# Attention steps woven between dense matmuls in a hybrid convolution and attention block on eight cores

## The chip, the cores and the metric

The kernel runs on all 8 cores of one Trainium2 chip, two dies of four cores. Each core computes one of the 8 sequences of the batch by itself; nothing is exchanged between cores. The metric is the device time of the slowest core in microseconds (us). Most executions agree within 0.3%, but this program also has a slower state, in which the cores of one die, or of both, show a lower granted TensorE clock.

Engines are called by their names, and in the profile by short ones: PE is TensorE's matmuls, PEld its weight loads, DVE is VectorE, ACT is ScalarE, POOL is GpSimd.

## The reference

```python
# x: (8, 4096, 1024) float32, one layer
h = rmsnorm(x) * g_mix
b, c, v, q, k, va, gc, ga = split(h @ w_in)          # 512 x 3, 512 x 3, 1024 x 2 columns
y_c = (b * causal_dwconv3(c * v)) @ w_conv_out
# differential attention: 4 heads, each two maps of 64-wide q/k and one 128-wide v
q, k = rope(rmsnorm(q)), rope(rmsnorm(k))
p0, p1 = softmax(mask(q0 k0' / 8)), softmax(mask(q1 k1' / 8))   # causal by chunks of 64
o = rmsnorm((p0 - lam * p1) @ va) * (1 - lam_init)
y_a = o @ w_attn_out
x = x + (sigmoid(gc) * y_c + sigmoid(ga) * y_a) @ w_o
x = x + swiglu(rmsnorm(x) * g_ffn)                   # 1024 -> 2816 -> 1024
```

## The kernel before

Rows go in eight tiles of 512. A tile runs stage by stage: norm, the input projection with the chains that normalise and rotate Q and K, attention, the output projection, feed-forward. Weights are cast from float32 in tile 0, written to device memory in bfloat16, and read from there in tiles 1 to 7. A small scheduler puts a semaphore wait wherever an instruction needs another engine's result; the order on each engine is the order in which the program emits.

Attention stands in one block per tile. For each of 4 heads and each 128-row key tile it issues two score matmuls of 64 rows, two Exps, two PV matmuls (the exponentials times V) with 512 query columns, a matmul with ones for one softmax sum, and a VectorE addition for the other:

```python
for n in range(2):
    S_.op("act", lambda n=n, pi=pi: nc.scalar.activation(
        out=Pb[:, pi, 0:N], in_=banks[sb0 + n][:, 0:N], func=AF.Exp, scale=0.125), ...)
# ... (the next scores but one are issued here)
for n in range(2):
    S_.op("pe", lambda n=n, pi=pi: nc.tensor.matmul(
        banks[n][:, qlo:T], lhsT=Vs[:, kt, h * 128:(h + 1) * 128], rhs=Pb[:, pi, 0:N], ...))
S_.op("pe", lambda p1=p1: nc.tensor.matmul(
    banks[B_L1][:, qlo:T], lhsT=ones[:], rhs=Pb[:, p1, 0:N], start=first, stop=last), ...)
# ... (Lacc[:, 0] += Pb[:, p0] on VectorE)
```

Eight PSUM banks serve everything in turn. The reciprocal square roots of the norms are Ln and Exp on ScalarE, silu and sigmoid are ScalarE functions too, so that activation tables are loaded 33 times.

## Time and profile before

| | before |
|---|---|
| time, median of 3 fast runs | 2957.18 us |
| TensorE busy, of a span of 2953.3 us | 2532.3 us (86%) |
| VectorE, ScalarE, GpSimd busy | 1304.6, 1212.2, 333.9 us |
| mean granted clock, both dies | 0.94 |
| activation table loads in all | 33 |

TensorE is the bound and has 421 us of holes. The prediction below shows them by stretch. The view of TensorE's waits names them (line waited with, what it waited for: us in all, times, longest):

```profile
PE bank L623 <- ACT Pb L637: 63.5, 48, 16.9
PE bank L371 <- DVE xn L361: 52.9, 28, 5.0
PE bank L728 <- DVE mixT L717: 46.2, 8, 6.8
```

These are scores waiting for Exp, transposes waiting for a normalised row, and the attention branch's mix at a stage border. No single one is large; all arise where one stage hands over to the next.

### The profile page before, as it was taken

What the parts mean: (1) busy time and instruction counts of PE and PEld (TensorE: products, weight loads), DVE (VectorE), ACT (ScalarE), POOL (GpSimd) and SP (SyncE); (2) the same over time, 40 slices, a digit from 0 to 9 for tenths busy, and PEclk for the clock granted to TensorE, in tenths of its full rate; (3) what the DMA queues carried; (4) which work ended last, traced back from release to release, by engine and by line L of the source; (5) the groups of instructions that cost most, each with busy time, mean ns of one, the idle gap of its engine ahead of it and who ended that gap; (6) DMA issues with size and microseconds to landing.
All of it is one profiled execution on the core that took longest, in us unless ns stands there. A gap on an engine that the chain in (4) does not pass through costs nothing.

```text
span 2953.3 us, 39312 instructions; the slowest of 8 cores (2940.4 to 2953.3 us)
## 1 busy us (share of the span) xinstructions
PE 2532.3 (86%) x11552; PEld 1036.5 (35%) x11552; DVE 1304.6 (44%) x2186; ACT 1212.2 (41%) x2355; POOL 333.9 (11%) x550
## 2 busy tenths in 40 slices
PE   3758778789887988889898898988989979899888
PEld 1323233244323433234332443223432234332244
DVE  4444234622555144731646225572164641446621
ACT  2453224521382216611385213872138921269620
POOL 1300013000400030000400004000040000400000
PEclk9878889999998999989999999999999989999999
DMA  6757974035312443025310353102531024430033
GB/s 203 253 174 242 327 271 153 33 114 193 123 71 72 170 172 115 27 102 187 140 73 30 116 208 123 53 30 104 187 138 72 1 80 169 165 115 1 29 114 143
DMA packets 58238, 376.06 MB, mean 127 GB/s; under 512 B 6448, under 2 KB 6576, under 8 KB 18352
## 3 DMA queue, kind: packets, MB, share of 16 engines
q1 hardware_dynamic: 44352, 307.49, 30.2%
q10 hardware_dynamic: 9216, 33.56, 3.3%
q0 software_dynamic: 4464, 32.51, 2.6%
q8 instruction: 100, 1.64, 0.2%
q14 instruction: 106, 0.87, 0.1%
HBM read 324.25 MB, written 49.28 MB: 126 GB/s over the span
## 4 chain that ended last, share of the span: by engine, by line
PE 56%; DVE 11%; issue 10%; ACT 8%; DMA 7%; POOL 7%; ACTq 0%; DVEq 0%; POOLq 0%; SPq 0%
PE bank L746 9%; PE bank L751 9%; PE bank L771 9%; PE bank L391 8%; PE bank L651 7%; DMA Vs<-wblk 6%; PE bank L623 5%; ACT Pb L637 5%; POOL scr L465 3%; PE bank L656 3%; PE bank L728 2%; DVE hT L373 2%; POOL scr L461 2%; PE bank L545 2%; DVE scr L714 1%
## 5 line engine op out<-in xcount | busy, mean ns | idle before, releaser
L637 ACT ACTIVATE Pb<-bank 128x512 bf16<-128x512 f32 (+3 forms) x1152 | 565.0, 564 | 49.7 <-PE bank L623 40.1
L663 DVE TENSOR_TENSOR Lacc<-Lacc,Pb 128x512 f32<-128x512 f32 (+3 forms) x544 | 350.8, 645 | 180.0 <-ACT Pb L637 127.0
L391 PE MATMUL bank<-hT,wring 128*128 128x512 bf16 x1792 | 398.8, 384 | 6.3 <-DVE scr L405 3.8
L746 PE MATMUL bank<-hT,wring 128*128 128x512 bf16 x1408 | 348.7, 392 | 22.4 <-DVE hT L373 12.8
L651 PE MATMUL bank<-Pb,Vs 128*128 128x512 bf16 (+3 forms) x1152 | 337.5, 376 | 11.3 <-POOL Pb L641 9.0
L751 PE MATMUL bank<-hT,wring 128*128 128x512 bf16 x1408 | 339.7, 385 | 0.0
L771 PE MATMUL bank<-wring,big 128*128 128x512 bf16 x1408 | 309.5, 381 | 17.1 <-ACT scr L755 7.9
L757 DVE TENSOR_TENSOR big<-bank,scr 128x512 bf16<-128x512 f32 x176 | 120.7, 691 | 453.5 <-PE bank L751 453.5
L623 PE MATMUL bank<-qT,kT 64*128 64x512 bf16 (+3 forms) x1152 | 248.6, 375 | 72.4 <-ACT Pb L637 63.5
L435 PE MATMUL bank<-wring,hT 128*128 128x512 bf16 x768 | 212.2, 433 | 83.1 <-DVE hT L373 23.5
L755 ACT ACTIVATE scr<-bank 128x512 f32<-128x512 f32 x176 | 104.1, 597 | 419.0 <-PE bank L746 418.9
L391 PEld LDWEIGHTS bank<-hT,wring 128*128 128x128 bf16 x1792 | 176.3, 99 | 220.4 <-issue 17.9
L656 PE MATMUL bank<-Pb,ones 128*128 128x512 bf16 (+1 forms) x576 | 212.7, 370 | 0.0
L746 PEld LDWEIGHTS bank<-hT,wring 128*128 128x128 bf16 x1408 | 140.0, 100 | 198.2 <-issue 41.6
L771 PEld LDWEIGHTS bank<-wring,big 128*128 128x128 bf16 x1408 | 137.7, 98 | 187.8 <-issue 25.4
L751 PEld LDWEIGHTS bank<-hT,wring 128*128 128x128 bf16 x1408 | 140.2, 100 | 174.5 <-issue 14.7
L623 PEld LDWEIGHTS bank<-qT,kT 64*128 64x128 bf16 x1152 | 66.2, 93 | 338.6 <-issue 334.1
L457 POOL TENSOR_TENSOR scr<-scr,tabs 128x256 f32<-128x256 f32 x64 | 46.5, 727 | 1151.5 <-DVE ss L452 1151.4
L728 PE MATMUL bank<-wring,mixT 128*128 128x512 bf16 x512 | 131.6, 419 | 46.2 <-DVE mixT L717 46.2
L435 PEld LDWEIGHTS bank<-wring,hT 128*128 128x128 bf16 x768 | 80.2, 109 | 188.5 <-issue 128.7
L641 POOL MEMSET Pb<- 64x64 bf16 x256 | 38.1, 151 | 943.4 <-ACT Pb L637 938.9
L351 ACT ACTIVATE xn<-xt 128x1024 bf16<-128x1024 f32 x36 | 38.0, 1056 | 241.8 <-DVE small L350 241.8
(110 smaller groups left out, 2237.5 us busy)
## 6 DMA issues: line engine op xcount, KB each, us to landing
wring<-wsc SPq DMA_DIRECT2D x217, 1024.0 KB, 5.4
Vs<-wblk SPq DMA_DIRECT2D x62, 1024.0 KB, 12.4
wsc<-wring POOLq DMA_DIRECT2D x31, 1024.0 KB, 12.0
out<-xt ACTq DMA_DIRECT2D x32, 512.0 KB, 7.4
Lacc<-x ACTq DMA_DIRECT2D x28, 512.0 KB, 4.3
xt<-x SPq DMA_DIRECT2D x28, 512.0 KB, 8.5
xt<-x ACTq DMA_DIRECT2D x4, 512.0 KB, 13.6
cst_sb<-cst SPq DMA_DIRECT2D x1, 232.0 KB, 5.6
```

The lines of the kernel that those rows point to most:

```text
L391: S_.op("pe", lambda kc=kc: nc.tensor.matmul(banks[bk][:], lhsT=wv[:, kc, c4 * 128:(c4 + 1) * 128], rhs=hT[:, kc, :], start=(kc == 0), sto ...
L435: S_.op("pe", lambda kc=kc: nc.tensor.matmul(banks[bk][:], lhsT=hT[:, kc, t * 128:(t + 1) * 128], rhs=wv[:, kc, :], start=(kc == 0), stop= ...
L623: S_.op("pe", lambda n=n: nc.tensor.matmul(banks[sb0 + n][:, 0:N], lhsT=kT[n * 64:(n + 1) * 64, h, kt * 128:(kt + 1) * 128], rhs=qT[n * 64 ...
L637: S_.op("act", lambda n=n, pi=pi: nc.scalar.activation(out=Pb[:, pi, 0:N], in_=banks[sb0 + n][:, 0:N], func=AF.Exp, scale=0.125), [("ps", ...
L651: S_.op("pe", lambda n=n, pi=pi: nc.tensor.matmul(banks[n][:, qlo:T], lhsT=Vs[:, kt, h * 128:(h + 1) * 128], rhs=Pb[:, pi, 0:N], start=fir ...
L656: S_.op("pe", lambda p1=p1: nc.tensor.matmul(banks[B_L1][:, qlo:T], lhsT=ones[:], rhs=Pb[:, p1, 0:N], start=first, stop=last), ["ones"] + ...
L663: S_.op("dve", lambda p0=p0: nc.vector.tensor_tensor(out=Lacc[:, 0, qlo:T], in0=Lacc[:, 0, qlo:T], in1=Pb[:, p0, 0:N], op=ALU.add), [("P", ...
L728: S_.op("pe", lambda kc=kc, t=t, bk=bk, wv=wv: nc.tensor.matmul(banks[bk][:], lhsT=mixT[:, kc, t * 128:(t + 1) * 128], rhs=wv[:, kc, :], s ...
L746: S_.op("pe", lambda kc=kc, c2=c2, bg=bg, wv=wv: nc.tensor.matmul(banks[bg][:], lhsT=wv[:, kc, c2 * 128:(c2 + 1) * 128], rhs=hT[:, kc, :], ...
L751: S_.op("pe", lambda kc=kc, c2=c2, bu=bu, wv=wv: nc.tensor.matmul(banks[bu][:], lhsT=wv[:, kc, 256 + c2 * 128:256 + (c2 + 1) * 128], rhs=h ...
L757: S_.op("dve", lambda bu=bu, sg=sg, fi=fi: nc.vector.tensor_tensor(out=big[:, fi, :], in0=banks[bu][:], in1=scr[:, sg, 0:T], op=ALU.mult), ...
L771: S_.op("pe", lambda kc=kc, kl=kl, t=t, c=c, bk=bk, wv=wv: nc.tensor.matmul(banks[bk][:], lhsT=big[:, kc, t * 128:(t + 1) * 128], rhs=wv[: ...
```

## The change

Its intent is to have no attention stage at all. The attention of tile j+1 is cut into steps of one key tile, and a step is put between the dense matmuls of the end of tile j and the start of tile j+1, whenever a credit that grows with every dense matmul reaches one. For that, Q, K and V of tile j+2 are computed in tile j. Chains of other engines (multiply, transpose) are not emitted at once but deferred by so many dense units, a unit being 4 to 8 dense matmuls into one bank.

```diff
+            def mm(fn, reads, writes):
+                S_.op("pe", fn, reads, writes)
+                if st["att"]:
+                    st["credit"] += st["rate"]
+                    while st["credit"] >= 1.0 and st["att"]:
+                        st["credit"] -= 1.0
+                        att_step()
...
+            def unit_end():
+                for e in later:
+                    e[0] -= 1
+                due = [e for e in later if e[0] <= 0]
...                                     # one Exp for both maps; one pair of score banks
-                                out=Pb[:, pi, 0:N], in_=banks[sb0 + n][:, 0:N], func=AF.Exp, scale=0.125),
+                    act(lambda: A.activation(out=Pb[:, pi, :, 0:N], in_=psS[:, :, 0:N], func=AF.Exp, scale=0.125),
...                                     # PV with the queries as rows and a 129th column of ones
-                                banks[n][:, qlo:T], lhsT=Vs[:, kt, h * 128:(h + 1) * 128], rhs=Pb[:, pi, 0:N],
+                                psO[:, b, s * VW:(s + 1) * VW], lhsT=Pb[:, pi, n, (q - r) * 128:(q - r + 1) * 128],
+                                rhs=Vs[:, kt, h * VW:(h + 1) * VW], start=(kt == 0 and s == 0), stop=(kt == 4 * j + q),
...                                     # norms: a power on GpSimd instead of Ln and Exp
+                pool(lambda: G.tensor_tensor(out=rs8, in0=ss8, in1=mhalf[:], op=ALU.pow), [("ss8", pb), "mhalf"], [("rs8", pb)])
...                                     # sigmoid and silu by tanh: one activation table set
-                            out=big[:, gi, :], in_=banks[bk][:], func=AF.Sigmoid,
+                act(lambda: A.activation(out=scr[:, th, 0:T], in_=psD[bk][:], func=AF.Tanh, bias=bgh[:, gi:gi + 1], scale=0.5),
...                                     # the head's epilogue (before fin: reciprocals, the two maps
...                                     # combined on VectorE into wv)
+                    for q in range(4):
+                        act(lambda q=q: A.activation(out=yq[:, yi, q * 128:(q + 1) * 128], in_=wv[:, q, :], func=AF.Square,
+                                                     accum_out=ss[:, q:q + 1]), [("scr", w)], [("yq", yi), ("ess", e)])
...
+                    defer(1, fin)
+                    defer(3, tr)
```

PSUM is divided: one pair of banks for scores, three banks for PV, three for all dense units and transposes. Weights come in half-blocks of 256 columns in place of whole blocks; 6 slots hold them in bfloat16, and 4 staging buffers hold the float32 loads of tile 0 until they are cast.

## The prediction

> **What bounds the kernel now.** I read the table of stretches first, one stretch per 512-row tile; the tile borders are where the chain of waits shows the first normalised rows of a tile being written.
>
> ```profile
> core 4: us, PE busy (x) PEld busy (x) DVE busy (x) ACT busy (x) POOL busy (x), PEclk, DMA share, GB/s
> 0.00:426.00 426.00, 276.43 (x1196) 118.83 (x1196) 167.77 (x276) 151.59 (x230) 57.59 (x102) 0.86 0.74 250
> 426.00:735.00 309.00, 270.19 (x1244) 116.45 (x1244) 129.11 (x226) 101.79 (x210) 39.50 (x64) 0.94 0.35 121
> 2538.00:2953.00 415.00, 372.25 (x1692) 144.24 (x1692) 192.68 (x314) 196.35 (x385) 39.24 (x64) 0.96 0.24 88
> ```
>
> Columns after the length: busy us and count of TensorE matmuls, weight loads, VectorE, ScalarE, GpSimd; granted clock; DMA share and rate. Tile 0 is another regime (DMA 0.74, clock 0.86). Tiles 1 to 7 grow from 309 to 415 us with attention. TensorE is the bound, idle for 2953.3 - 2532.3 = 421 us. The last tile by stage shows where:
>
> ```profile
> 2538.00:2590.00 52.00, 41.12 (x188) 18.20 (x188) 29.59 (x61) 16.73 (x43) 34.53 (x32) 0.91 0.35 130
> 2627.00:2778.00 151.00, 143.63 (x650) 42.88 (x651) 97.05 (x148) 141.52 (x280) 4.70 (x32) 0.99 0.02 7
> 2792.00:2829.00 37.00, 23.51 (x116) 10.51 (x115) 21.61 (x34) 6.22 (x16) 0.00 (x0) 0.84 0.26 96
> 2829.00:2906.00 77.00, 77.00 (x345) 34.39 (x346) 14.53 (x21) 13.82 (x22) 0.00 (x0) 0.97 0.39 137
> ```
>
> Q/K/V (52 us) and output projection (37) have holes and a low clock; attention (151) is ScalarE's, busy 141.5; gate/up (77) is solid, 352 matmuls at 216 ns. Cut into 10 us pieces, the clock is 1.00 except just behind a hole:
>
> ```profile
> 2826.00:2836.00 10.00, 8.04 (x29) 3.51 (x30) 3.05 (x4) 1.88 (x2) 0.00 (x0) 0.59 0.01 2
> 2836.00:2846.00 10.00, 10.00 (x48) 4.51 (x46) 1.72 (x4) 1.79 (x3) 0.00 (x0) 1.00 0.27 105
> ```
>
> Tile 0's late stretch is a chain of weight loads (start, us, what), at a saturated DMA of 330 GB/s (last line, from the table of stretches):
>
> ```profile
> 334.14 13.96 DMA Vs<-wblk
> 348.24 1.91 ACT wring L329
> 350.21 12.46 DMA Vs<-wblk
> ...
> 340.00:380.00 40.00, 26.46 (x110) 10.98 (x109) 8.50 (x10) 10.58 (x11) 2.13 (x4) 0.83 0.99 330
> ```
>
> For the cost of small matmuls and of Exp I read the timeline and the groups by shape:
>
> ```profile
> 1060.30 0.61 PE L371 MATMUL bank<-ident,xn 128*128 128x128 bf16 x8 [0.19 <-DVE xt L779]
> 2700.68 0.65 PE L623 MATMUL bank<-qT,kT 64*128 64x512 bf16 x4
> L637 ACT ACTIVATE Pb<-bank 128x512 bf16<-128x512 f32 x960 | 504.5, 600 | 38.1 <-PE bank L623 35.5 <-DVE Lacc L663 1.3 <-ACT Pb L637 0.8
> L637 ACT ACTIVATE Pb<-bank 128x128 bf16<-128x128 f32 x64 | 14.6, 277 | 9.5 <-PE bank L623 4.6 <-POOL Pb L641 4.1
> L426 ACT ACT_TABLE_LOAD x8 | 10.3, 1283 | 56.3 <-PE bank L391 56.3
> ```
>
> Eight transposes, each with its own weight load, take 0.61 us; less one latency of 219 ns that is 391/7 = 56 ns apiece. Four 64-row QK matmuls take 0.65 us, less 387 ns latency: the fourth starts 0.26 us after the first, so a pair overlaps.
>
> **What the Trainium skill says.**
> - "TensorE: Matmul & The Clock Gate", Back-to-back issue gap: about 81 ns per matmul of 128 columns in a stream with weight loads, 56 ns isolated. The trace has 56 with loads; I use 56.
> - The same page, What's actually happening and Seeing it yourself: the clock halves after about 3.4 us idle, and with three dense cores on a die it falls to 13/16. The trace agrees with the first (0.59 behind a hole) and not the second (1.00 on eight cores).
> - "ScalarE: Activation LUTs", What ACT_TABLE_LOAD costs and Table sets: 186 ns + 0.833 ns per element, 1283 ns per load, exp and tanh in one set. The trace: (600 - 277)/384 = 0.84 ns, 1283 ns. No run yet shows the shared set.
> - "HBM Reference", Specifications: about 358 GB/s per core; the trace tops out near 330.
>
> **The change part by part.**
>
> *TensorE work at full clock.* Dense matmuls stay 976 x 8 = 7808, at 215.7 ns: 1684 us. Removed: the ones matmul of each key tile (480 of 512 columns, 32 each of 384, 256, 128: about 114 us), the fp32 row sum (32 x 0.9 = 29) and the ones matmul of the norm (7), 150 in all. PV turns from 1152 wide matmuls (960 x 0.216 + 64 x (0.162 + 0.109 + 0.056) = 228) into 3584 + 640 = 4224 of 129 columns, at 56 ns 237. QK pairs are now always issued together: 480 x 0.26 (216 ns, and part of the 63 ns by which the second of a pair starts late) + 32 x 0.46 (the three diagonal shapes) = 140. Transposes: 512 + 256 + 128 new ones = 896 x 0.056 = 50. Sum 1684 + 140 + 237 + 50 = 2111 us.
>
> *ScalarE.* One Exp covers both maps: 171 + 0.84 x 1024 = 1.03 us against 2 x 0.6, and 552 us in all (480 x 1.03, 32 x 1.8 for the three diagonal shapes). With the rest (tanh 192, norms and squares 177, copies 115, casts 59) some 1095 us; 32 table loads (41 us) go. No longer a bound, because the Exp is spread over the dense matmuls: in the worst tile, 131 steps over 736 matmuls, one every 5.6. A step plus its dense share is 0.73 + 1.21 = 1.94 us of TensorE, while the single score pair comes free after 0.28 + 0.24 + 1.10 = 1.62 us. Only a tanh in between breaks that: about 15 us in all.
>
> *VectorE.* The row-sum adds (351 us) go; the silu gets a second pass (176 x 0.75 = 132), down is evicted in 192 pieces instead of 64 (+96), the epilogue about 110. I get about 1190 us, 53%: not a bound on average, but in bursts.
>
> *Tile 0 and its prefetch.* 62 half-blocks of 1 MB plus 0.5 MB written back: 1.57/0.328 = 4.8 us each against 3.45 us of matmuls. Setup until the sine tables have gone through DRAM: 42 us. Q/K/V of tiles 0 and 1, paced by VectorE: 2 x 30. Then 52 half-blocks x 4.8 = 249, x tiles 13, bf16 reloads 10, and 10 lost while tile 2's Q/K/V holds the four staging buffers. Together 384, say 385 us. In it TensorE does 1168 dense matmuls (252), attention 0 and most of 1 (24), transposes (13): 289 us.
>
> *The other seven tiles.* 2111 - 289 = 1822 us. At a clock of 0.975 (holes are smaller than now, when tiles show 0.94 to 0.96) 1869 us.
>
> *Stalls that remain.* Three dense banks instead of eight, and VectorE in program order. Per tile with a look-ahead: four normalised transposes ahead of the output projection, evicted at 1.2 us each, 2.5 us; residual and norm, then eight Q/K units of 3.1 us VectorE each (plus 4.9 for the FFN norm) against 2.5 us of TensorE, 10 us; conv taps (3.7 us each) and four norms ahead of the first gated unit, 5.5 us. That is 18, five times outside tile 0: 90. The last two tiles have no Q/K/V to hide the FFN norm: 13 each, 26. With the score pair's 15: 131 us.
>
> *Tail*, last evictions and store: 9, as now. Sum: 385 + 1869 + 131 + 9 = 2394 us, or 0.81 of before.
>
> **The rivals.**
> - *Small PV matmuls cost more than 56 ns* (the skill's 81, or waits on P). For: P is fresh, and weight load and matmul are the same length. Against: the transposes. It adds 4224 x 25 ns = 106 us: 2500.
> - *VectorE becomes the bound*: its bursts and the tiny GpSimd powers, unmeasured, hold the banks. At 2 us a power in norm chains, about 80 more: 2475.
> - *The clock falls* because TensorE is never quiet. Against: 77 us solid at 1.00. At 13/16 the seven tiles would take 1822/0.8125 = 2243: 2770.
> - *Bursts are absorbed* by banks and woven attention, and tile 0 runs nearer its bytes (110 MB at 328 GB/s, 335 us): 345 + 1840 + 60 + 9 = 2254.
> - *Tile 0 is hidden anyway*: then only the weaving counts, and the gain is within these numbers.
>
> **Range and chances.** The fast corner is 2254; stalls of 220 and a clock of 0.95 give about 2540. I take 2270 to 2520. Even the throttled case is 6% faster than 2957, so faster is nearly certain, short of a wait I have missed on the single score pair.
>
> **What would show it right or wrong.** Ones matmuls and row-sum adds gone; PV at about 56 ns start to start; Exp near 1.03 us on 576 instructions; table loads down to a handful; TensorE busy above 93% behind tile 0 with a clock near 0.975; tile 0 ending near 385 us with DMA at 0.9 or more; holes of 10 us in Q/K/V and of 5 at the conv-to-gate border. It is wrong if the clock sits near 0.81, if PV runs at 80 ns, if tile 0 takes over 430 us, or if the waits on VectorE exceed 200 us.

## The result, and the profile after

The changed kernel takes 2863.55 us by the median of four executions. One of these was slow (3089.83); the fast ones are 2845.6, 2860.79 and 2866.3. Ratios here are the mean time of one kernel's fast runs over that of the other's of the same rounds, so not quite the ratio of the medians: 0.966, with a 95% interval of 0.962 to 0.970. It is faster, by 3.4% instead of the predicted 19%; 2394 us and the range up to 2520 were far off.

The page's line of busy times, changed kernel:

```profile
PE 2393.0 (84%) x14080; PEld 1110.5 (39%) x14080; DVE 1159.1 (41%) x2138; ACT 1058.7 (37%) x1556; POOL 243.5 (9%) x239
```

TensorE's work fell by 139 us, and its share fell too: the holes grew from 421 to 451 us. The groups by shape show that the instructions are what they were taken for (count, busy us, mean ns):

```profile
L606 ACT ACTIVATE Pb<-psS 128x1024 bf16<-128x1024 f32 x480 | 490.8, 1023 | 649.0 <-PE psS L600 640.2 <-DVE xt L803 3.0 <-DVE big L829 1.8
...
L411 ACT ACT_TABLE_LOAD x1 | 1.3, 1283 | 7.6 <-DMA xt<-x 7.6
L470 ACT ACT_TABLE_LOAD x1 | 1.3, 1283 | 0.5 <-ACT big L456 0.5
```

One Exp over both maps takes 1.023 us, and two table loads are left. The table of stretches, by tile (length, busy us of TensorE, its weight loads, VectorE, ScalarE, GpSimd, clock, DMA share, GB/s):

```profile
0.00:548.00 548.00, 359.74 (x1757) 159.38 (x1758) 262.26 (x482) 191.05 (x281) 82.22 (x81) 0.86 0.63 204
548.00:868.00 320.00, 275.88 (x1495) 124.83 (x1493) 138.66 (x260) 97.94 (x164) 30.33 (x29) 0.92 0.38 128
...
1910.00:2270.00 360.00, 318.27 (x2112) 151.68 (x2110) 138.64 (x260) 159.72 (x225) 30.33 (x29) 0.97 0.32 106
```

Tile 0 takes 548 us where 385 had been predicted, and its DMA share is 0.63 where 0.9 or more had been. The later tiles have holes and, with them, a clock of 0.92 to 0.97. The waits of TensorE:

```profile
PE psD L666 <- DVE yq L657: 76.0, 19, 5.6
PE psS L600 <- ACT Pb L606: 58.9, 25, 7.6
PE psD L555 <- DVE scr L538: 54.2, 29, 3.4
PE psD L515 <- DVE scr L538: 46.2, 16, 5.1
```

L666 are the transposes that end a head's attention epilogue (its softmax sums divided out, the two maps combined, the row normalised and transposed), L600 the scores, L555 and L515 the transposes and the projection in the Q/K/V stages. All waits for VectorE together are 373 us by this view, against 248 before.

To put these in relation I added up the gaps from one matmul's start to the next on the slowest core: content at full clock (215.8 ns for 512 columns, 56 for 128 and so on), the part of the rest that a lowered clock explains, and waits. Content is 2089 us, clock loss 143, waits 596. The prediction had 2111 of content and 283 for all else; 2089 counts a pair of scores as one matmul, 2111 had 0.26 us for it, which is about the difference. Of the two runs in the last columns the next section tells.

| clock loss and waits, us | predicted | changed kernel | epilogue spread | best |
|---|---|---|---|---|
| tile 0 (with the first Q/K/V stages) | 96 | 249 | 224 | 171 |
| Q/K/V, borders, output projection, tiles 1 to 7 | 116 | 310 | 283 | 174 |
| feed-forward and convolution stages, tiles 1 to 7 | 15 | 180 | 107 | 109 |
| clock, not divided by place | 47 | (above) | (above) | (above) |
| sum | 274 | 739 | 614 | 454 |

The predicted 96 is 385 less 289 of content, 116 is 90 for the look-ahead tiles and 26 for the last two; the tail's 9 is left out of the column.

**Two chains read from the timeline.** The first is the end of a head in tile 2's down projection (start us, us, engine, line):

```profile
1187.26 0.39 PE L600 MATMUL psS<-qT,kT 64*128 64x512 bf16 x2
...
1192.75 0.58 PE L666 MATMUL psD<-ident,yq 128*128 128x128 bf16 x4 [3.92 <-DVE yq L657]
...
1188.43 0.31 ACT L650 ACTIVATE yq<-scr 128x128 bf16<-128x128 f32 x1 [2.74 <-DVE scr L645]
...
1190.22 1.00 ACT L606 ACTIVATE Pb<-psS 128x1024 bf16<-128x1024 f32 x1
...
1190.80 1.01 POOL L654 TENSOR_TENSOR ep<-ep,mhalf 128x4 f32<-128x4 f32 x1 [61.74 <-DVE ep L652]
...
1191.91 0.69 DVE L657 TENSOR_TENSOR yq<-scr,ep 128x512 bf16<-128x512 f32 x1 [0.33 <-POOL ep L654]
```

ScalarE stands 2.74 us in front of the first square (L650), because VectorE is still combining the two maps. The Exp of the scores of 1187.26 is behind the four squares in program order and starts at 1190.22. GpSimd's power ends at 1191.81, VectorE's multiply starts 0.1 us later, and TensorE, which met the transposes (L666) three units after the epilogue, has stood still for 3.92 us. The clock is then reduced: 0.67 in the 4 us that follow, in the table of stretches. The head shown is typical: in the view of ScalarE's waits it stands before the first square at 31 of the 32 heads.

```profile
ACT yq L650 <- DVE scr L645: 104.8, 31, 6.3
```

The second is a Q/K unit of tile 1 on VectorE:

```profile
139.15 0.68 DVE L529 TENSOR_TENSOR scr<-psD,tabs 128x512 f32<-128x512 f32 x1
...
140.61 0.68 DVE L538 TENSOR_TENSOR scr<-psD,tabs 128x512 f32<-128x512 f32 x1
143.70 0.69 DVE L546 TENSOR_TENSOR yq<-scr,st 128x512 bf16<-128x512 f32 x1 [2.41 <-POOL scr L542]
144.31 0.68 DVE L529 TENSOR_TENSOR scr<-psD,tabs 128x512 f32<-128x512 f32 x1
```

The unit's pitch is 144.31 - 139.15 = 5.16 us, of which VectorE stands 2.41 in front of L546, waiting for GpSimd's power (1.64 us) and addition (1.09). The reason is a count: the chain says "after one unit", but it is registered before its own unit ends, so that the multiply is emitted at the end of the same unit.

### The profile page after: what moved, and what is told of

It reads as the page before. It is cut to its first block, busy times and chain, and to the rows that moved or that the text cites. A ratio compares the mean times of both kernels' runs of the same rounds, so it can differ in the third digit from the quotient of the medians.

```text
span 2843.8 us, 41548 instructions; the slowest of 8 cores (2839.7 to 2843.8 us)
## 1 busy us (share of the span) xinstructions
PE 2393.0 (84%) x14080; PEld 1110.5 (39%) x14080; DVE 1159.1 (41%) x2138; ACT 1058.7 (37%) x1556; POOL 243.5 (9%) x239
## 4 chain that ended last, share of the span: by engine, by line
PE 67%; DVE 13%; issue 8%; ACT 4%; POOL 4%; DMA 3%; DVEq 1%; ACTq 0%; POOLq 0%; SPq 0%
PE psD L817 20%; PE psD L698 12%; PE psO L617 10%; PE psD L844 9%; PE psS L600 6%; PE psD L515 4%; PE psD L764 4%; PE psD L791 3%; DMA kT<-wblk 2%; ACT yq L650 2%; POOL scr L542 2%; DVE scr L645 2%; DVE scr L529 2%; DVE st L532 1%; POOL small L415 1%
## 5 line engine op out<-in xcount | busy, mean ns | idle before, releaser
L606 ACT ACTIVATE Pb<-psS 128x1024 bf16<-128x1024 f32 (+1 forms) x576 | 548.1, 952 | 795.5 <-PE psS L600 774.8
L817 PE MATMUL psD<-hF,wring 128*128 128x512 bf16 x2816 | 666.3, 385 | 10.5 <-DVE hF L426 5.0
L698 PE MATMUL psD<-hT,wring 128*128 128x512 bf16 x1792 | 448.0, 395 | 15.9 <-DVE Pb L609 6.9
L817 PEld LDWEIGHTS psD<-hF,wring 128*128 128x128 bf16 x2816 | 267.0, 99 | 294.0 <-issue 30.1
L617 PE MATMUL psO<-Vs,Pb 128*128 128x129 bf16 x4224 | 351.7, 229 | 3.1 <-DVE Pb L609 3.1
L844 PE MATMUL psD<-wring,big 128*128 128x512 bf16 x1408 | 333.3, 383 | 8.3 <-DVE wring L356 7.7
L515 PE MATMUL psD<-wring,hT 128*128 128x512 bf16 x768 | 245.5, 468 | 76.2 <-DVE scr L538 46.2
L617 PEld LDWEIGHTS psO<-Vs,Pb 128*128 128x128 bf16 x4224 | 256.1, 101 | 123.6 <-issue 114.7
L803 DVE SCALAR_TENSOR_TENSOR xt<-psD,xt 128x512 f32<-128x512 f32 x256 | 176.2, 691 | 272.3 <-PE psD L844 214.7
L600 PE MATMUL psS<-qT,kT 64*128 64x512 bf16 (+3 forms) x1152 | 222.1, 382 | 59.0 <-ACT Pb L606 58.9
L600 PEld LDWEIGHTS psS<-qT,kT 64*128 64x128 bf16 x1152 | 56.3, 93 | 315.5 <-issue 315.5
L515 PEld LDWEIGHTS psD<-wring,hT 128*128 128x128 bf16 x768 | 81.4, 114 | 175.1 <-issue 135.2
L791 PE MATMUL psD<-wring,big 128*128 128x512 bf16 x512 | 124.7, 392 | 7.5 <-DVE wring L356 3.6
## 6 DMA issues: line engine op xcount, KB each, us to landing
xt<-x ACTq DMA_DIRECT2D x4, 512.0 KB, 13.6
```

Of the source, the lines that this page charges most:

```text
L515: mm(lambda kc=kc, k4=k4, wv=wv: nc.tensor.matmul(psD[bk][:], lhsT=hT[:, jb, kc, t * 128:(t + 1) * 128], rhs=wv[:, k4, :], start=(kc == 0) ...
L600: S_.op("pe", lambda n=n: nc.tensor.matmul(psS[:, n, 0:N], lhsT=kT[n * 64:(n + 1) * 64, h, kt * 128:(kt + 1) * 128], rhs=qT[n * 64:(n + 1) ...
L606: act(lambda: A.activation(out=Pb[:, pi, :, 0:N], in_=psS[:, :, 0:N], func=AF.Exp, scale=0.125), [("ps", "S")], [("P", pi)])
L617: S_.op("pe", lambda q=q, n=n, b=b, s=s: nc.tensor.matmul(psO[:, b, s * VW:(s + 1) * VW], lhsT=Pb[:, pi, n, (q - r) * 128:(q - r + 1) * 12 ...
L698: mm(lambda kc=kc: nc.tensor.matmul(psD[bk][:], lhsT=wv[:, kc, col * 128:(col + 1) * 128], rhs=hT[:, jb, kc, :], start=(kc == 0), stop=(kc ...
L791: mm(lambda kc=kc, k4=k4, wv=wv, t=t, bk=bk: nc.tensor.matmul(psD[bk][:], lhsT=mixT[:, kc, t * 128:(t + 1) * 128], rhs=wv[:, k4, :], start ...
```

## The experiments

All give correct results but the one that is wrong. "Changed kernel" stands for its fast runs, 2846 to 2866 us, mean 2858.

**The Q/K chain's multiply one unit later.**

```diff
-                defer(1, fin)
-                defer(3, tr)
+                defer(2, fin)
+                defer(4, tr)
```

> Only the Q/K finishing multiply (and its transposes) are put one unit later. In the changed kernel a Q/K unit takes 5.2 us: VectorE runs four operations (0.69+0.68+0.17+0.69), then stands 2.4 us at the finishing multiply until GpSimd has done the power (1.64) and the add (1.1), then 0.69. Theory A (this chain in VectorE's program order is what the Q/K/V stage costs): the pitch falls to about 3.2 us, each of the eight Q/K/V stages of some 62 us to about 42, the first two included, so 2845 becomes 2690 +- 30. Theory B (the three dense banks, which the transposes share, bound the stage anyway): the pitch stays over 4.5 us and the time over 2800. Theory C (tile 0's time is its weight loads, hidden anyway): tiles 1 to 7 gain but tile 0 stays at 548.

Measured: 2766.57 and 2774.24 us (a third run, slow, 2906.32), ratio to before 0.936. VectorE's multiply now follows without a gap:

```profile
138.27 0.68 DVE L538 TENSOR_TENSOR scr<-psD,tabs 128x512 f32<-128x512 f32 x1
138.87 0.68 DVE L546 TENSOR_TENSOR yq<-scr,st 128x512 bf16<-128x512 f32 x1
```

By the places of the matmuls in the traces, the Q/K/V stages of the later tiles went from between 62 and 66 us to between 47 and 51, and the first two together from 129 to 108. So the cause is real, worth 87 us, and about half as large as expected: in these stages TensorE then waited for banks whose evictions stood behind other work of VectorE.

**The norms of the tile after next spread over the gate units.**

```diff
-                        norm_pre(t)
-                for t in range(4):
-                    x_load(j, t)
+                        defer(2 + 3 * t, lambda t=t: (norm_pre(t), x_load(j, t)))
```

> Only the four look-ahead norms, which stand together behind the conv, are spread over the first gated stage, one every three units. In the changed kernel that stage takes 38 us for 23 us of matmuls in tiles 1 to 5. Theory A (VectorE waits in program order for ScalarE's squares and GpSimd's powers, and the gated units' banks wait behind it): the stage falls to about 30 us, 6 x 8 = 50 us in all, so about 2795. Theory B (the stage's holes come from the last head's transposes and the conv taps): under 15 us gain.

Measured: 2850.66 us (and 2900.19, 1.7% above it). A miss: no gain, although the border between convolution and gate had 14 us of waits and clock loss a tile. In its place the trace showed the last head's transposes at that border, 5.5 to 6.1 us, and the convolution taps.

**The weaving undone, all else kept.** After each start of an attention its steps are run one behind the other.

```diff
+                while st["att"]:
+                    att_step()
+                    unit_end()
```

> The weaving undone: all attention steps of a tile one after the other at the same place of the program, everything else as in the changed kernel. A step then costs the loop of the single score pair, about 0.28 + 0.24 + 1.1 = 1.65 us against 0.93 us of TensorE now. Theory (weaving is what carries the gain): 448 full steps x 0.75 us and 128 short ones x 0.4 more, so about 2845 + 390 = 3235, slower than the kernel before. Rival (ScalarE's Exp total is what counts, woven or not, so the stage is as in the kernel before at 1.05 us a step): about 2900.

Measured: 3417.55 us, one run, far slower than the kernel before and 180 us more than the theory expected. The first line of the waits says why:

```profile
PE psS L600 <- ACT Pb L606: 460.5, 509, 6.3
```

With one pair of score banks each step waits for the Exp of the step ahead. So the change's cheaper attention (query-major PV, one Exp) loses without the weaving, and the weaving is worth some 560 us in this kernel with its single pair. Part of that may be order: the edit counts each step as a unit, so that the deferred chains come due among the steps.

**Scores over the full 128 rows, wrong** (both maps' products are added; the result is off by 0.34 relative). It tests whether the step of 0.89 us, predicted as 0.73, comes from the change between 64-row and 128-row matmuls. In the changed kernel a step looks like this:

```profile
1163.88 2.97 PE L844 MATMUL psD<-wring,big 128*128 128x512 bf16 x13
1166.78 0.39 PE L600 MATMUL psS<-qT,kT 64*128 64x512 bf16 x2
1167.10 0.63 PE L617 MATMUL psO<-Vs,Pb 128*128 128x129 bf16 x8
1167.56 2.75 PE L844 MATMUL psD<-wring,big 128*128 128x512 bf16 x12
```

Thirteen dense matmuls at 0.216 us would be through at 1166.69; the scores start 0.1 us later, and PV 0.32 us behind them instead of 0.22.

```diff
-                            psS[:, n, 0:N], lhsT=kT[n * 64:(n + 1) * 64, h, kt * 128:(kt + 1) * 128],
-                            rhs=qT[n * 64:(n + 1) * 64, jb, h, qlo:T], start=True, stop=True),
+                            psS[:, n, 0:N], lhsT=kT[:, h, kt * 128:(kt + 1) * 128],
+                            rhs=qT[:, jb, h, qlo:T], start=True, stop=True),
```

> Wrong results on purpose: the two score matmuls of a step use all 128 rows instead of 64 each (so both maps get the sum of both scores), which takes the pair's overlap away (2 x 216 ns) but also the change between 64-row and 128-row matmuls. Theory A (that change costs about 0.1 us into and 0.1 us out of every pair, as the gaps before the first score matmul and after the second suggest): the two cancel, a step keeps its 0.9 us, total within 30 us of 2845. Theory B (the gaps are waits for the Exp): a step grows by about 0.15 us, 448 steps, total about 2910.

Measured: 2865.17 us, one run, within the stated 30 us: theory A. In its trace the second score matmul starts 216 ns after the first, where it was 3 ns, so the overlap is gone, and yet a full step takes 0.89 us by the median of 364, as in the changed kernel. The overlap of the 64-row pair gains about what the change of shape costs.

**The epilogue's transposes later.** In the epilogue the multiply is emitted one unit later, the transposes after five units instead of three.

```diff
-                    defer(1, fin)
-                    defer(3, tr)
+                    defer(2, fin)
+                    defer(5, tr)
```

> One edit to the changed kernel: the attention epilogue's normalising multiply is emitted at the end of the next unit and its four transposes after five units instead of three. Theory A (the transposes are reached by TensorE before VectorE, ScalarE and GpSimd have finished the head's normalisation; the waits of 76 us 'transposes waiting for yq' and the clock loss behind them are real time): those waits fall below 20 us and the run ends near 2790 us, 2770 to 2815. Theory B (VectorE is behind anyway, so the wait only moves to the next bank that it must evict): within 15 us of the changed kernel's 2846 to 2866.

Measured: 2813.33 and 2815.68 us fast (two more slow), ratio to before 0.952. The 76 us of waits at the transposes left the list's first eleven places (below 11.5 us), and the time fell by 43 us: theory A, at the upper edge of its range. The scores still waited 54 us for Exp.

**Each gate unit one ahead of its branch unit.**

```diff
+                    if dc < 7:
+                        ths.append(gate(j, HB_GC, 0, dc + 1))
+                    branch(j, HB_CO, 0, dc, ths[dc])
```

> One edit to the changed kernel: each gate unit (8 matmuls, 1.73 us) is issued one ahead of the branch unit that it multiplies, so that one more gate unit stands between the last convolution taps and the first matmul that reads them, and between the last head's transposes and the first matmul that reads those. Theory A (the border waits are a fixed latency of VectorE, so 1.73 us of cover comes straight off): 8 tiles x 2 borders x up to 1.73 us, 20 to 28 us less, near 2832. Theory B (what TensorE meets there is the last head's own transposes, issued at the end of a unit wherever that stands): within 10 us of 2855.

Measured: 2862.29, 2862.46 and 2863.24 us fast (three more slow), no gain: theory B. The transposes wait at the end of a unit wherever that stands.

**The norm's multiply two units behind its power, the feed-forward norm's transposes among the V units**, on top of the later Q/K multiply.

```diff
-                            norm_pre(t)
-                            defer(5, lambda t=t: norm_T(t, C_GFFN, hF, "hF"))
+                            norm_pre(t, 2)
+                            defer(11, lambda t=t: norm_T(t, C_GFFN, hF, "hF"))
...                                     # and for the norm of tile 1, in tile 0
-                defer(2 + t, lambda t=t: norm_pre(t))
-                defer(6 + t, lambda t=t: norm_T(t, C_GMIX, hT[:, 1], hkey(1)))
+                defer(2 + t, lambda t=t: norm_pre(t, 1))
+                defer(9 + t, lambda t=t: norm_T(t, C_GMIX, hT[:, 1], hkey(1)))
```

> On top of the run that moved the Q/K chain's last multiply one unit later (2767 to 2774 us): the norm's own multiply is emitted two units after its small GpSimd power, and the feed-forward norm's transposes, which each occupy a bank until VectorE's 1.2 us eviction, are moved from the Q and K units to the V units. Theory A (in the Q/K/V stages VectorE stands still for GpSimd in program order, and the norm's evictions fall into its busiest units): the first Q/K/V stage falls from 71 to under 60 us, the later ones from 47 to about 40, and the whole to 2715, 2695 to 2735. Theory B (VectorE's 29 us of work in such a stage are themselves the bound, wherever they stand): within 15 us of 2770.

Measured: 2723.64 us (the other two are over 2% slower), 47 us less than the run beneath it: theory A by the sum, but not by its parts. The first two Q/K/V stages together fell from 108 to 88 us, 20 of the 47; each later one lost only about 2 us and stayed at 46 to 50, where about 40 had been expected. So most of what shows is tile 0's part of the edit, and how much belongs to the multiply standing still for GpSimd and how much to the evictions in the wrong place was not tried.

**Tile 0's casts on GpSimd**, also on the later Q/K multiply.

```diff
+                if k >= 6:
+                    pool(lambda: G.tensor_copy(dst, sv), stg_keys(i), [("w", sl)])
```

> On top of the same run (2767 to 2774 us): in tile 0 the 56 casts of weights behind the first six go to GpSimd instead of ScalarE and VectorE. Theory A (a cast that waits for its 1 MB load blocks the Exp, tanh and evictions queued behind it in program order, and that is why tile 0 is 90 us longer than predicted although the DMA is not full): tile 0 ends 20 to 40 us earlier, 2730 to 2755. Theory B (tile 0 is limited by the loop load, cast, free staging buffer, and GpSimd casts at 3 us or more instead of 1.2 to 1.9): 2775 to 2830.

Measured: 2765.0 us (two more slow), 5 us less than the mean of the run beneath it, so outside both ranges and in effect nothing. GpSimd casts a half-block in 2 us, about as long as ScalarE's 1.9:

```profile
L354 POOL CAST wring<-kT 128x2048 bf16<-128x2048 f32 x30 | 59.7, 2000 | 44.1 <-DMA kT<-wblk 33.1 <-PE psS L602 7.8 <-PE psO L619 3.1
```

Taking the casts out of ScalarE's and VectorE's order is therefore not enough to shorten tile 0, which ended some 7 us earlier. That the casts, for whose loads GpSimd then waited 62.5 us (33.1 in this line, 29.4 for the other two buffers), held up GpSimd's powers instead is not ruled out.

**Four edits together** (later Q/K multiply, later norm, later epilogue, gate ahead, as shown above), and tile 1's sine table loaded early.

```diff
+            defer(2, lambda: load_cs(1))
             proj_qkv(0, False)
-            load_cs(1)
```

> Four edits together on the changed kernel: the Q/K chain's last multiply a unit later, the norm's multiply and the feed-forward norm's transposes later, the attention epilogue's transposes later, each gate unit one ahead, and besides these tile 1's sine table loaded a Q/K/V stage earlier. Theory A (these are separate waits that add up): 2721 us of the run with the first two, less 43 for the epilogue, less 10 for the table, less up to 10 for the border now that the transposes no longer stand in it: 2660, 2640 to 2685. Theory B (each wait removed lets TensorE run into the next one of VectorE's backlog): 2690 or more.

Measured: 2687.44 and 2689.44 us fast (a third, 2722.86, slow). The parts add up to 2724 - 43 - 10 = 2671, and 17 of that were not got. It lies between the two ranges, nearer B's: the scores still waited 44 us for Exp.

**The epilogue's squares a unit later**, on top of the last.

```diff
-                    for q in range(4):
-                        act(lambda q=q: A.activation(... func=AF.Square, ...
+                    def sq():
+                        for q in range(4):
+                            act(lambda q=q: A.activation(... func=AF.Square, ...
...
+                    defer(2, sq)
-                    defer(2, fin)
+                    defer(3, fin)
                     defer(5, tr)
```

The sum and the power behind the squares go with them, and the multiply moves a unit too.

> The kernel with these edits, and one more: the epilogue's four squares on ScalarE, which wait for VectorE's combination of the two maps, are emitted a unit later instead of straight behind it. Theory A (ScalarE, in program order, stands still at those squares until VectorE is done, with the next Exp queued behind them; this is the 50 to 59 us of 'scores waiting for Exp', up to 8 us each): that wait falls below 20 us and the time by 30 to 60 us from the run without it. Theory B (the single score pair itself is what TensorE waits for, Exp taking 1.02 us a step): within 15 us of the run without it.

Measured: 2598.4 us fast (a second, slow, 2815.44): 90 us less, more than theory A allowed. The wait of scores for Exp fell from 44 to 11 us, and ScalarE's before the squares from 120 to 47.

**The norms spread once more**, on top of that; the same edit had brought nothing by itself.

```diff
+                        defer(2 + 3 * t, lambda t=t: (norm_pre(t), x_load(j, t)))
```

> One more edit on top: the four norms of the tile after next, with the loads behind them, are spread over the gate units instead of standing in a row ahead of the first one (without the other edits this brought nothing). Theory A (the last head's transposes hid it then; now it is exposed): 15 to 30 us less than the run without it. Theory B (VectorE is drained at this border anyway): within 10 us.

Measured: 2560.48 and 2561.49 us, ratio to before 0.865 (0.863 to 0.867): 37 us less, beyond theory A's range. The border was covered by the transposes before; now it is exposed, and the edit counts. This is the best version, 13.5% faster than the kernel before and 10% faster than the changed kernel. Its stretches for tile 0, tile 1 and tile 4, and below them its two first waits of TensorE:

```profile
0.00:471.00 471.00, 341.24 (x1760) 151.95 (x1761) 264.21 (x482) 190.10 (x281) 87.68 (x81) 0.92 0.72 236
471.00:759.00 288.00, 265.18 (x1491) 122.37 (x1489) 138.72 (x260) 97.76 (x163) 32.39 (x29) 0.96 0.44 145
...
1360.00:1677.00 317.00, 301.44 (x1980) 143.99 (x1978) 139.46 (x261) 145.25 (x212) 32.40 (x29) 0.99 0.36 123
```

```profile
PE psD L519 <- DVE scr L542: 57.3, 25, 5.1
PE psD L428 <- DVE xn L417: 33.0, 9, 12.3
```

Tile 4 is at a clock of 0.99. What is left waits in the Q/K/V stages (L519) and at the start (L428).

**V units between Q and K units**, on top of the best.

```diff
-                for hbs, kind in ((HB_Q, 0), (HB_K, 1), (HB_V, 2)):
-                    for t in range(4):
+                for kind, t in ((0, 0), (0, 1), (2, 0), (0, 2), (0, 3), (2, 1), (1, 0), (1, 1), (2, 2), ...
```

> One more edit on top: in the Q/K/V stages a V unit, which needs nothing of VectorE, follows each two Q or K units, instead of four V units at the end, and the feed-forward norm's transposes come one to each such group. Theory A (the banks wait because VectorE's 29 us of work are packed into two thirds of the stage): 4 to 6 us less in each of seven stages, 25 to 40 us in all. Theory B (holding four weight blocks instead of two starves the loads for the next stage, or VectorE's sum is the bound): within 10 us, or slower. In sum A for all four would end near 2560 us, 0.865 of before.

Measured: 2588.07, 2588.95 and 2591.94 us fast (a fourth, slow, 2647.32), 29 us slower: theory B. The projection's wait for VectorE's eviction grew from 57 to 71 us. The edit also moves the norm transposes of tile 1, and 11 of the 29 us came in the first two Q/K/V stages; the later ones gained nothing either. Whether the held weight blocks or VectorE's sum is to blame was not separated.

**The squares alone, at the end of their unit, on the changed kernel.**

```diff
+                    defer(1, sq)
                     defer(1, fin)
                     defer(3, tr)
```

> The changed kernel with one edit alone: the epilogue's squares, with the sum and the power behind them, are emitted at the end of the unit instead of straight behind VectorE's combination of the two maps; the last multiply and the transposes keep their places. Theory A (the squares hold up the Exp behind them in ScalarE's order, whatever else waits): the wait of scores for Exp falls from 59 to below 30 us, and the run ends near 2815 us, 2800 to 2835, against 2846 to 2866. Theory B (on this kernel the transposes, 76 us of waits, then wait longer by the same amount, because squares moved back make the normalised rows later): within 15 us of 2855.

Measured: 2853.87 us (a second run, 2909.14, is slow). By its number it is B, but not by B's reason: scores still waited 54 us and transposes 77, both nearly as without the edit. The end of the unit mostly still comes before VectorE's combination is done: ScalarE's waits before the squares fell only from 105 to 90 us.

**Squares after two units, multiply after three, transposes after five, on the changed kernel and nothing else.**

> The changed kernel with the whole epilogue spread and nothing else: squares after two units, last multiply after three, transposes after five. Theory A (this chain across three engines is the largest single cause of the miss): 43 us of the transposes alone and 90 of the squares in the ladder add up on the changed kernel as well: near 2725 us, 2705 to 2755. Theory B (the 90 us came out only because the other edits stood beneath it): 2780 or more.

Measured: 2721.02 us (three more were slow, but the undisturbed die of each had spans of 2704 to 2723 us, as the fast run's cores had 2707 to 2719): theory A, 137 us less than the changed kernel.

```profile
PE psS L600 <- ACT Pb L606: 13.8, 19, 1.4
...
PE psD L668 <- DVE yq L659: 13.6, 9, 1.9
```

Scores went from 58.9 to 13.8 us of waits, transposes from 76.0 to 13.6, together 107; ScalarE's waits before the squares fell from 105 to 35 us, and the clock loss from 143 to 100. This is the largest single cause found. In the table above it takes 73 us out of the feed-forward and convolution stages, for which the prediction had only 15 us of stalls in all.

## Why the prediction was wrong

**TensorE's content: right.** 2089 us against 2111, and the same when a pair of scores is counted alike. The PV matmuls run at 57 ns start to start (eight in 0.63 us less one latency of 0.23), so the rival of 80 ns fell. Dense matmuls and transposes were as counted.

**ScalarE and VectorE totals, and the table loads: right.** 1059 us against 1095, 1159 against 1190, Exp 1.023 against 1.03 us, two loads where 33 had been. Totals were not what went wrong. VectorE's is in part luck, or at least not shown: the terms that the prediction gives lead from 1304.6 to 1292 and not to 1190, and 1190 is 50% of 2394, not 53%.

**The clock: the mechanism right, the size off.** The rival of 13/16 fell for the fast state: tile 4 of the best version holds 0.99 on eight cores. 0.975 had been predicted and 0.93 came, as there were more holes than predicted for it to fall behind (0.67 behind the one shown above). It rose to 0.95 with the epilogue spread alone and to 0.97 in the best version, without anything being done about the clock.

**"Only a tanh in between breaks that: about 15 us in all": failed; this is the largest term.** The step compared TensorE's 1.94 us per step with the 1.62 us until the score pair is free, and assumed that ScalarE turns to an Exp as soon as it comes. The epilogue had been counted as "about 110" us of VectorE work. It is a chain through VectorE, ScalarE, VectorE, GpSimd, VectorE and TensorE, 8 us from the first reciprocal to the transposes in the head shown above. Emitted at once, its squares stop ScalarE, for 105 us in all, with the next Exp behind them, and its transposes, due after three units, stop TensorE. Spreading it took off 137 us.

**"eight Q/K units of 3.1 us VectorE each [...] 10 us": failed.** The work is right, about 3 us, but the pitch is 5.2, since the multiply was emitted in its own unit and VectorE stood 2.4 us for GpSimd. I had read the deferral as the next unit. The stage's 10 us of stalls became 32, clock included. The later multiply took off 87 us, and the norm's multiply and transposes together 47 more, of which 20 in tile 0. The rival "its bursts and the tiny GpSimd powers" named this mechanism and was near with the power (1.64 us for 2 assumed), but charged it 80 us as a latency, where it was an engine standing still.

**"conv taps (3.7 us each) and four norms ahead of the first gated unit, 5.5 us": mis-sized, and hidden.** It was 14 us a tile. Two edits there gained nothing on their own, because the last head's transposes stood in the same place; once those and the squares were out of the way, one of them gained 37 us.

**"A step plus its dense share is 0.73 + 1.21": the step is mis-sized.** It takes 0.89 us for 0.73: by the medians of all 576 steps in the trace the scores start 0.096 us late behind a dense matmul, and PV 0.103 late behind the scores. 576 steps x 0.16 = 92 us. The full-row run agrees, and of the best version's 109 us in the feed-forward and convolution stages these gaps are about four fifths, by the place where they stand. The prediction had left out a sentence of the Trainium skill that bears on it: "TensorEngine Tiling (Array Packing)", Key Properties, says that changing the tiling mode drains TensorE. The trace agrees, at about 0.1 us each way.

**"Together 384, say 385 us", tile 0: failed, in part still open.** It took 548. The two first Q/K/V stages took 73 and 55 us instead of 30 each; in the best version 52 and 37. From there on the sum took 4.8 us for each half-block, as if the loads always ran; in the Q/K/V stages the DMA share fell to 0.4 and less. A load waits for a free staging buffer, that for a cast, and the cast for a slot which TensorE must release, so a hole of TensorE becomes a hole of the DMA. That is how the program is written, and it fits that tile 0 fell to 471 us, by edits none of which concerned the loads except for the sine table. (The DMA share's rise from 0.63 to 0.72 shows nothing more: 0.63 x 548 and 0.72 x 471 are both some 340 us of transfers.) The casts' place alone is not the cause. Of the 86 us that remain over the prediction, 29 are in the first two Q/K/V stages. For the rest the waits in tile 0 of the best version point to the weights: TensorE stood 49 us there for casts, and ScalarE 56 us for the loads that it was to cast. No run tests it, so this part stays open.

Together: of a miss of some 460 us, 297 came back by edits of order alone (2858 to 2561), and the remaining 167 are 86 in tile 0 and 81 behind it, about as much as the 92 of the steps, though the two were not measured against each other. The stated signs that would make the prediction wrong, tile 0 over 430 us and waits for VectorE over 200 us, are the two that came; but the second could not tell much, since these waits were 248 us in the kernel before.

## What to carry to other kernels

When work of several engines is woven, count for each engine not its busy time but what it stands in front of: an instruction whose input comes from another engine blocked, in these traces, everything emitted behind it on its own engine, so it belongs as many units later as its chain takes. Read a deferral in the program as closely as a duration in the profile, since one unit off cost 87 us here. An edit that gains nothing may only be covered by another wait in the same place; try it again once that one is gone.

## What the Trainium skill lacked or had wrong

- "TensorE: Matmul & The Clock Gate", Back-to-back issue gap, gives about 81 ns for 128 columns in a stream with weight loads. Here 129 columns with a fresh weight load each took 57 ns.
- The same page, Seeing it yourself, lets three dense cores of a die fall to 13/16. Fast runs here do not: 0.99 over a whole tile of 317 us on eight cores. But slow runs of the same programs show all four cores of a die low together (0.78 to 0.79 beside 0.92 on the other die, in a run of the kernel with the gate unit ahead). Whether that is the page's limit is open, as no trace of a slow run was kept.
- "TensorEngine Tiling (Array Packing)", Key Properties, names the drain at a change of tiling mode without a figure. Here it is about 0.1 us each way between 64-row and 128-row matmuls, enough to use up the gain of the overlapping pair.
- "GPSIMD Engine Reference" has an addition but no power. Here a power (a tensor to the elementwise power of another) over 128 rows with 1, 4 and 8 columns took 0.55, 1.01 and 1.64 us.
- "ScalarE: Activation LUTs", Table sets, puts exp and tanh in one set and copy in every set, and does not say where square is. Here exp, tanh, copy and square ran among each other with two table loads in all.
